# Reordering the hybrid layer's last attention units and the start of the first MLP in a two-layer diffusion backbone

## The chip, the cores and the metric

One Trainium2 chip, and of it one core. The metric is the device time of one execution in microseconds (us): a median over runs of the same program. A profile is one further execution with its own time. PE is TensorE (matmul), DVE is VectorE, ACT is ScalarE, POOL is GpSimd, SP is SyncE, whose queue issues most of the loads.

## What is computed

Two post-norm layers over 512 latent tokens and 256 context tokens, all in float32, model width 1024. Layer 0 is a hybrid mixer: one input projection, a bidirectional state-space scan (16 heads in 4 groups, chunks of 128 tokens) beside neighbourhood attention (8 heads), one output projection. Layer 1 is differential attention. Each layer then has a gated MLP with a convolution of width 3.

```python
ox, oc = hybrid_mixer(ux, uc, ...)            # layer 0: scan || attention, then w_out
hx = layer_norm(ALPHA * hx + mx[2] * ox, ln1_g, ln1_b)
fx = conv_ffn(modulate(hx, mx[3], mx[4]), w_up, conv_w, conv_b, w_down)
hx = layer_norm(ALPHA * hx + mx[5] * fx, ln2_g, ln2_b)

def conv_ffn(u, w_up, conv_w, conv_b, w_down):
    hdn = dwconv_centred(u @ w_up, conv_w, conv_b)
    val, gate = jnp.split(hdn, 2, axis=-1)
    return (jax.nn.silu(gate) * val) @ w_down
```

The shift, scale and gate vectors mx come from a vector times `ada_w` (1024 by 6144 in each layer).

## The kernel before

**Precision.** Each dense product is made of three passes in a reduced float format: a weight is loaded raw, split by `wchunk` (L152) into a high part `whi` (ACT, L172) and a low part `wlo` (raw minus high, L173, on DVE or, where `eng` is given, on POOL), and PE adds high times high, high times low and low times high. So a product over 1024 channels is 24 matmuls.

**Order.** The program is written as one stream. A planner at compile time gives each engine a fixed order: of the instructions that are ready by its own clock it takes the one written earliest, unless `tc.cur_priority` was raised around it (plus 4000 means: only when nothing else is ready; `ADA_LATER`, 100, a little later). On the chip each engine then works through its own queue in that order. Where `pe.chain` is true, each PE instruction that goes through `pe` is also tied behind the one written before it.

**Hybrid layer.** Before the loop over groups stand `dense_ssd(0)`, `dense_z(0)`, `x_rows(0)` (L878). The loop at L930 runs for g = 0 to 3; `run` (L857) alternates the generators `ssd_group(g)` (scan of group g: 12 steps, the last six one for each chunk) and `na_pair(g-1)` (six attention units of one head pair), and takes one step of a filler list in every second round: the dense work of the next group, `dense_na(g)`, `dense_z(g+1)`, for g = 3 also `early()` (transposes of finished scan rows by `prep_y`, and the first two output tiles `po`). For g = 3 the filler has priority plus 4000. `dense_z(g)` makes the gate z of group g: 6 tiles of 24 matmuls of 128x256; the last operation of each chunk in `ssd_group` (L709) multiplies by it.

An attention unit is: scores S (two heads, PE), softmax (DVE, ACT, DVE), transposes of P (PE), copies (ACT), product with V (PE). `split_qk` and `na_values` prepare Q, K and V of a pair in one buffer each.

After the loop come `rr` (the scan's RMS factor, L949 to L952), the gate rows G, and a part with an order written out by hand: the six units of pair 3 alternate with `piece()`, one step of `rest()`, which is an output tile `po` of 18 matmuls in the first ten steps. Each unit there is split in three: scores, transposes, product. Then follow the rest of the output projection and `out_att` (L996), with the layer norm.

**First MLP.** `ffn` (L1067) has 11 groups of two `up` calls each (an `up` is two weight chunks, two products for the latent and two for the context tokens, conv3 on ACT and DVE, gate, split) and `down`, which adds the product of a group to the residual Y (ev on DVE, L350, the sum on POOL, L352). Group gi = 1 also runs the affine maps of the first layer norm on the six tiles of Y (`affine`, L406, 8 POOL operations each), and `bgstep` interleaves `ada_dve` (L208): the modulation vectors of later sub-layers, accumulated on DVE (acc, L223) from 512 KB loads on the SP queue. In the kernel before, `bgstep(STEPS0)` takes five steps after each `up` of group 1 and two after later ones, `down` lags one group behind `up` until the last groups, where it lags two, and `W_POOL` puts the low parts of chunks 4 to 9 on POOL (chunk 2j+i belongs to `up(j)`).

## Time and profile before

| what | us |
|---|---|
| median of 3 runs (2025.8 to 2028.28) | 2026.2 |
| profiled execution | 2025.07 |
| its span, first to last instruction | 2023.3 |
| PE busy | 1920.8 |
| DVE busy | 1352.1 |
| ACT busy | 920.5 |
| POOL busy | 769.6 |

In the span the hybrid layer lasts to about 675, the first MLP to about 1235, the second layer's attention to about 1650, the second MLP to the end. A line of the timeline gives the start and the duration, engine, source line, operation, out<-in, shape and count; in square brackets stands the idle time of the engine before it and what ended it. S<-nKh,nQ are scores, S<-c_consts,P transposes, S<-Pt,V products with V.

### The profile page before, as it was taken

What the parts mean: (1) busy time and instruction counts of PE and PEld (TensorE: products, weight loads), DVE (VectorE), ACT (ScalarE), POOL (GpSimd) and SP (SyncE); (2) the same over time, 40 slices, a digit from 0 to 9 for tenths busy, and PEclk for the clock granted to TensorE, in tenths of its full rate; (3) what the DMA queues carried; (4) which work ended last, traced back from release to release, by engine and by line L of the source; (5) the groups of instructions that cost most, each with busy time, mean ns of one, the idle gap of its engine ahead of it and who ended that gap; (6) DMA issues with size and microseconds to landing.
All of it is one profiled execution on the core that took longest, in us unless ns stands there. A gap on an engine that the chain in (4) does not pass through costs nothing.

```text
span 2023.3 us, 31146 instructions
## 1 busy us (share of the span) xinstructions
PE 1920.8 (95%) x11928; PEld 1645.3 (81%) x11928; DVE 1352.1 (67%) x2172; ACT 920.5 (45%) x1799; POOL 769.6 (38%) x658
## 2 busy tenths in 40 slices
PE   7998999998699889999999999899999899999997
PEld 5887889887477788878888888899998788888886
DVE  3757565765556887887676667566665876655566
ACT  3545466585442732323222234656665644333332
POOL 2135224336315675444444408431115264222133
PEclk9999999999699989999999999999999999999999
DMA  9335342233422243433343342222122223323321
GB/s 314 113 114 170 110 129 76 96 117 117 155 68 88 87 135 100 130 116 115 105 144 106 104 135 86 92 73 85 55 66 68 89 64 126 104 84 104 103 96 62
DMA packets 109445, 217.59 MB, mean 108 GB/s; under 512 B 27112, under 2 KB 45904, under 8 KB 109296
## 3 DMA queue, kind: packets, MB, share of 16 engines
q1 hardware_dynamic: 95168, 187.87, 28.9%
q0 software_dynamic: 6016, 20.03, 2.8%
q10 hardware_dynamic: 8112, 7.71, 1.3%
q8 instruction: 94, 1.54, 0.3%
q14 instruction: 55, 0.45, 0.1%
HBM read 202.81 MB, written 8.55 MB: 104 GB/s over the span
## 4 chain that ended last, share of the span: by engine, by line
PE 72%; DVE 12%; DMA 4%; POOL 4%; ACT 4%; issue 3%; ACTq 0%; SPq 0%; DVEq 0%; POOLq 0%
PE fpx L328 20%; PE pdn L1122 11%; PE px L328 7%; PE fpc L328 5%; PE S L108 3%; PE po L108 3%; PE pc L328 3%; PE pz L344 3%; DVE acc L223 2%; PE pv L344 2%; DMA araw<-in_ada_w 2%; POOL y L409 2%; PE dSp L1329 2%; PE po L1005 2%; PE pk L328 2%
## 5 line engine op out<-in xcount | busy, mean ns | idle before, releaser
L172 ACT ACTIVATE whi<-raw 128x1024 fp32r<-128x1024 f32 (+1 forms) x203 | 213.4, 1056 | 443.5 <-PE fpc L328 167.2
L173 DVE TENSOR_TENSOR wlo<-raw,whi 128x1024 fp32r<-128x1024 f32 (+1 forms) x190 | 251.8, 1330 | 157.4 <-ACT whi L172 144.6
L352 POOL TENSOR_TENSOR y<-y,ev 128x512 f32<-128x512 f32 x144 | 212.5, 1495 | 185.1 <-DVE ev L350 175.2
L1122 PE MATMUL pdn<-whi,fact 128*128 128x512 f32 x880 | 273.1, 392 | 2.1 <-DVE ev L350 1.8
L328 PE MATMUL fpx<-ux,whi 128*128 128x512 f32 (+1 forms) x832 | 232.3, 363 | 8.2 <-DVE cv L1081 7.6
L328 PE MATMUL fpx<-u,whi 128*128 128x512 f32 (+1 forms) x832 | 226.5, 358 | 2.4 <-DVE cv L1081 1.5
L1122 PEld LDWEIGHTS pdn<-whi,fact 128*128 128x128 f32 x880 | 162.4, 188 | 37.2 <-DVE ev L350 2.9
L328 PEld LDWEIGHTS fpx<-ux,whi 128*128 128x128 f32 x832 | 150.3, 194 | 31.1 <-ACT whi L172 8.0
L1122 PE MATMUL pdn<-wlo,fact 128*128 128x512 f32 x440 | 170.8, 390 | 0.7 <-DVE wlo L173 0.7
L328 PEld LDWEIGHTS fpx<-u,whi 128*128 128x128 f32 x832 | 149.2, 191 | 25.1 <-ACT cv L1077 1.6
L328 PE MATMUL fpx<-ux,wlo 128*128 128x512 f32 (+1 forms) x416 | 151.1, 364 | 8.5 <-POOL wlo L173 6.6
L223 DVE SCALAR_TENSOR_TENSOR acc<-araw,condp,acc 128x512 f32<-128x512 f32 x140 | 137.4, 1002 | 24.4 <-DMA araw<-in_ada_w 24.0
L1106 POOL TENSOR_TENSOR fact<-cv,fact 128x768 fp32r<-128x768 f32 (+1 forms) x44 | 70.6, 1605 | 217.5 <-ACT fact L1105 217.5
L328 PE MATMUL fpx<-u,wlo 128*128 128x512 f32 (+1 forms) x416 | 148.8, 358 | 1.1 <-DVE wlo L173 1.1
L328 PE MATMUL px<-ux,whi 128*128 128x512 f32 x448 | 148.5, 405 | 0.0
L171 POOL TENSOR_TENSOR raw<-raw,G 128x1024 f32<-128x1024 f32 x30 | 74.4, 2482 | 193.0 <-DMA raw<-in_w_down 113.0
L1081 DVE SCALAR_TENSOR_TENSOR cv<-fpx,fcw,cv 128x511 f32<-128x511 f32 x176 | 130.3, 744 | 20.8 <-ACT cv L1077 19.6
L328 PE MATMUL fpc<-uc,whi 128*128 128x256 f32 x704 | 130.2, 283 | 0.0
L328 PEld LDWEIGHTS fpc<-uc,whi 128*128 128x128 f32 x704 | 112.6, 191 | 4.2 <-issue 0.6
L409 POOL TENSOR_TENSOR y<-y,gb 128x256 f32<-128x256 f32 x112 | 98.9, 918 | 35.2 <-PE lntp L388 28.7
L1077 ACT ACTIVATE cv<-fpx,fcw 128x512 f32<-128x512 f32 x88 | 67.8, 771 | 80.7 <-PE fpx L328 76.5
L350 DVE SCALAR_TENSOR_TENSOR ev<-pdn,G 128x512 f32<-128x512 f32 x120 | 81.3, 683 | 32.0 <-POOL y L352 18.9
(335 smaller groups left out, 4628.0 us busy)
## 6 DMA issues: line engine op xcount, KB each, us to landing
araw<-in_ada_w SPq DMA_DIRECT2D x96, 512.0 KB
raw<-in_w_up SPq DMA_DIRECT2D x88, 512.0 KB
raw<-in_w_down SPq DMA_DIRECT2D x44, 512.0 KB
E<-scr POOLq DMA_DIRECT2D x24, 512.0 KB, 5.4
raw<-in_w_dqk SPq DMA_DIRECT2D x16, 512.0 KB
raw<-in_w_qkv SPq DMA_DIRECT2D x12, 512.0 KB
raw<-in_w_out SPq DMA_DIRECT2D x12, 512.0 KB
raw<-in_w_bc SPq DMA_DIRECT2D x8, 512.0 KB
```

The lines of the kernel that those rows point to most:

```text
L108: i = f(*a, **k)
L171: nc.gpsimd.tensor_tensor(raw, raw, gate, op=OP.mult)
L172: nc.scalar.activation(hi[:, :n], raw[:, :n], AF.Copy)
L173: i = (eng or nc.vector).tensor_tensor(lo[:, :n], raw[:, :n], hi[:, :n].bitcast(F32), op=OP.subtract)
L223: nc.vector.scalar_tensor_tensor(acc[:, s], raw[:, i], cs, acc[:, s], op0=OP.mult, op1=OP.add)
L328: nc.tensor.matmul(ps, w[wi][:, kc], rhs(kc, ui), start=(i == 0), stop=(i == n - 1))
L344: nc.tensor.matmul(ps, u_dst(u, kc, ui, tt), w(kc, wi), start=(i == 0), stop=(i == n - 1))
L350: nc.vector.scalar_tensor_tensor(t, ps, r, Gh, op0=OP.mult, op1=OP.mult)
L352: eng.tensor_tensor(yh, yh, t, op=OP.add)
L409: i = nc.gpsimd.tensor_tensor(y[:, c:c + 256], y[:, c:c + 256], t[:, c:c + 256], op=op)
L1081: nc.vector.scalar_tensor_tensor(dst[:, lo:hi_], src[:, lo + d:hi_ + d], f[:, tap:tap + 1], dst[:, lo:hi_], op0=OP.mult, op1=OP.add)
L1122: nc.tensor.matmul(ps, acts[2 * gs[0] + kt][:, ui, 128 * tt:128 * tt + 128], ws[kt][wi][:, 0, o:o + 512], start=(m == 0), stop=(m == 3 * n ...
```

## The change

`dense_z(g)` moves from the end of the filler of group g-1 to the head of the filler of group g (for group 0 from the part ahead of the loop). `rr` is computed inside the last chunk step of group 3. In group 3 `na_pair` makes only units 0 to 2 of pair 2; units 3 to 5 go, split in three, to the head of the order written by hand, and `QK3` and `V3` of pair 3 are made after them. Two output tiles stand between the three units, two more before and after the scores of pair 3's first unit. In the first MLP `down` lags two groups throughout, the affine maps are written three after each `up` of group 1, `bgstep` takes three steps after each `up` of groups 1 to 3, G is made in group 2, and the chunks whose low part POOL makes are 8 to 11 in place of 4 to 9.

```diff
--- before.py
+++ after.py
@@ -44,11 +44,9 @@
 
 E_AHEAD = (0, 1, 1, 2)
 
-STEPS0 = 5
-
 ADA_LATER = 100
 
-W_POOL = ((4, 5, 6, 7, 8, 9), (4, 6, 8))
+W_POOL = ((8, 9, 10, 11), (4, 6, 8))
 D_POOL = (0, 1)
 DO_POOL = (0, 1)
 OB_POOL = (2, 4)
@@ -147,7 +145,6 @@
     W = (wf, "w")
     wring = [W]
     wcount = [0]
-    pool_wlo = [None]
 
     def wchunk(src, shape, gate=None, eng=None, rows=None, rp=None):
         n = int(np.prod(shape))
@@ -170,9 +167,7 @@
         if gate is not None:
             nc.gpsimd.tensor_tensor(raw, raw, gate, op=OP.mult)
         nc.scalar.activation(hi[:, :n], raw[:, :n], AF.Copy)
-        i = (eng or nc.vector).tensor_tensor(lo[:, :n], raw[:, :n], hi[:, :n].bitcast(F32), op=OP.subtract)
-        if eng is not None:
-            pool_wlo[0] = i
+        (eng or nc.vector).tensor_tensor(lo[:, :n], raw[:, :n], hi[:, :n].bitcast(F32), op=OP.subtract)
         return [t[:, :n].rearrange("p (a b) -> p a b", a=shape[0]) for t in (hi, lo)]
 
     def wrows(src, n, shape, eng=None):
@@ -709,6 +704,11 @@
             nc.vector.tensor_tensor(yf, yf, zs.pop((g, c)), op=OP.mult)
             nc.gpsimd.dma_start(scrY[c, :, 256 * g:256 * g + 256], yf)
             nc.scalar.activation(t1[:, 0].rearrange("p h q -> p (h q)"), yf, AF.Square, accum_out=ssq[:, c, g:g + 1])
+            if g == 3 and c == 3:
+                ssr = sp.tile([128, 6], F32, name="ssr")
+                nc.vector.tensor_reduce(ssr, ssq, axis=AX, op=OP.add)
+                nc.vector.tensor_scalar(ssr, ssr, 1.0 / D, RMS_EPS, op0=OP.mult, op1=OP.add)
+                nc.vector.tensor_scalar(rr, rsqrt_(ssr, sp), 1.0 / ALPHA, None, op0=OP.mult)
             yield
 
 
@@ -816,6 +816,8 @@
                 pe.matmul(av[hp], V[0:m, c, hp], Ss[e][1][0:m, i], start=(i == 0), stop=(i == len(chunks) - 1))
         out(av)
 
+    held = {}
+
     def na_values(v):
         V = np_.tile([128, 7, 128], F32, name="V")
         for grp in ((1, 2, 3, 5), (6, 0, 4)):
@@ -844,11 +846,12 @@
             return na_unit(*QK, V, 128 * k, k0, chunks + (5, 6), bt, lambda av: na_out(p, 128 * k, av), pool, tp_, nb, split)
         return na_unit(*QK, V, 128 * k, None, (5, 6), None, lambda av: na_out(p, 128 * k, av), pool, tp_, nb, split)
 
-    def na_pair(p, q, k, v, pools, nb=2):
+    def na_pair(p, q, k, v, pools, nb=2, n=6):
         QK = split_qk(q, k)
         V = na_values(v)
+        held[p] = QK, V
         yield
-        for u_ in range(6):
+        for u_ in range(n):
             bt = na_bias(p, u_, np_, nb) if u_ < 4 else None
             for _ in na_one(p, u_, QK, V, bt, pools[u_ % 4 % len(pools)], np_, nb):
                 pass
@@ -875,7 +878,7 @@
     PNA = (pna, "na")
     dense, densen, rows, zs = {}, {}, {}, {}
     bg[:] = [(0, w, h) for w in (2, 4, 3) for h in range(2)]
-    for _ in chain(dense_ssd(0), dense_z(0), x_rows(0)):
+    for _ in chain(dense_ssd(0), x_rows(0)):
         pass
     acts, atts, Yt, pend = {}, {}, {}, []
 
@@ -932,13 +935,11 @@
             pmm.seq = MM
         gens = [ssd_group(g, *rows[g])]
         if g > 0:
-            gens.append(na_pair(g - 1, *densen[g - 1], [(nring, None) if g == 3 else PNA]))
-        fl = []
+            gens.append(na_pair(g - 1, *densen[g - 1], [(nring, None) if g == 3 else PNA], n=3 if g == 3 else 6))
+        fl = [dense_z(g)]
         if g < 3:
             fl += [dense_ssd(g + 1), x_rows(g + 1)]
         fl.append(dense_na(g))
-        if g < 3:
-            fl.append(dense_z(g + 1))
         if g == 3:
             fl.append(early())
         run(gens, chain(*fl), 4000 if g == 3 else 0)
@@ -946,10 +947,6 @@
     pmm.seq = MM + [(pm3, "mm")]
     while bg:
         fill()
-    ssr = sp.tile([128, 6], F32, name="ssr")
-    nc.vector.tensor_reduce(ssr, ssq, axis=AX, op=OP.add)
-    nc.vector.tensor_scalar(ssr, ssr, 1.0 / D, RMS_EPS, op0=OP.mult, op1=OP.add)
-    nc.vector.tensor_scalar(rr, rsqrt_(ssr, sp), 1.0 / ALPHA, None, op0=OP.mult)
     s1.close()
     s4 = ExitStack()
     op4 = s4.enter_context(tc.tile_pool(name="op4", bufs=1))
@@ -1026,22 +1023,33 @@
         next(rs_, None)
         tc.cur_priority = pr
 
+    two = (PNA, (pss, "ax"))
+    bt2 = na_bias(2, 3, np_, 2)
+    late = [lambda k=k: na_one(2, k, *held[2], bt2 if k == 3 else None, two[k % 2], np_, 2, True) for k in (3, 4, 5)]
     bts = [na_bias(3, b, np2, 4) for b in range(2)]
-    QK3 = split_qk(*N[:2])
-    V3 = na_values(N[2])
     for tt in range(6):
         load_res(tt)
     evac_y()
     pe.chain = True
     prev = None
-    for k in range(6):
+    for n_, make in enumerate(late + list(range(6))):
+        if n_ == 3:
+            next(prev)
+            piece()
+            next(prev, None)
+            prev = None
+            QK3 = split_qk(*N[:2])
+            V3 = na_values(N[2])
+            piece()
+        k = n_ - 3
         if 0 < k < 3:
             bts.append(na_bias(3, k + 1, np2, 4))
-        un = na_one(3, k, QK3, V3, bts[k] if k < 4 else None, (PNA, (pss, "ax"))[k % 2], np2, 4, True)
+        un = make() if n_ < 3 else na_one(3, k, QK3, V3, bts[k] if k < 4 else None, two[k % 2], np2, 4, True)
         next(un)
         if prev is not None:
             next(prev)
-        piece()
+        if n_:
+            piece()
         if prev is not None:
             next(prev, None)
         prev = un
@@ -1174,20 +1182,18 @@
         if not pieces:
             G = [gate_rows(l, 1, 0, fL, "G0")]
             wring[:] = [W, W, W, W, (arp, "ar")]
+        lag = 2 if with_ctx else 1
         for gi in range(1, NG):
             for i in range(2):
                 up(2 * gi + i, 2 if gi < 2 else 1)
-                if gi == 1 and i == 0 and with_ctx:
-                    for tt in range(3):
-                        affine(Y[tt], gb, pool_wlo[0] if tt == 0 else None)
-                bgstep(STEPS0 if gi == 1 else 2)
-            if gi == 1 and pieces:
+                if gi == 1 and with_ctx:
+                    for tt in range(3 * i, 3 * i + 3):
+                        affine(Y[tt], gb)
+                bgstep(3 if gi <= 3 else 2)
+            if gi == 2 and pieces:
                 G = [gate_rows(l, 1, s, fL, f"G{s}", scaled=False) for s in range(2)]
-            if gi < NG - 2:
-                if gi == 1 and with_ctx:
-                    for tt in range(3, 6):
-                        affine(Y[tt], gb)
-                down([gi - 1])
+            if lag <= gi < NG - 3 + lag:
+                down([gi - lag])
                 bgstep(1)
         down([NG - 3])
         wring[:] = [W]
```

## Rows read from the trace of the kernel before

**Rows 1.** The page: busy time of each engine, and the clock in 40 slices.

```profile
PE 1920.8 (95%) x11928; PEld 1645.3 (81%) x11928; DVE 1352.1 (67%) x2172; ACT 920.5 (45%) x1799; POOL 769.6 (38%) x658
PEclk9999999999699989999999999999999999999999
```

**Rows 2.** Windows: length, busy us (and count) of engines, PE clock, DMA share, GB/s.

```profile
336.00:442.00 106.00, 104.31 (x698) 90.99 (x697) 72.96 (x165) 69.89 (x161) 39.55 (x52) 1.00 0.31 98
...
442.00:485.00 43.00, 42.98 (x270) 36.88 (x269) 21.45 (x41) 27.64 (x68) 17.69 (x21) 1.00 0.27 89
485.00:531.00 46.00, 36.55 (x177) 27.84 (x175) 28.56 (x66) 25.19 (x72) 28.38 (x37) 0.78 0.55 186
531.79:560.05 28.26, 14.81 (x66) 8.67 (x67) 16.57 (x29) 14.47 (x42) 7.46 (x4) 0.57 0.31 100
560.05:607.20 47.15, 47.06 (x274) 35.88 (x272) 26.51 (x62) 18.98 (x54) 9.47 (x8) 0.97 0.21 66
...
675.24:768.89 93.65, 78.12 (x624) 76.37 (x624) 73.52 (x90) 40.41 (x75) 67.88 (x58) 0.91 0.37 118
```

**Rows 3.** Windows of the same columns, cut where the granted clock is half.

```profile
535.74:563.04 27.30, 16.02 (x61) 9.92 (x60) 18.56 (x34) 13.12 (x37) 7.46 (x4) 0.50 0.29 96
...
702.99:713.23 10.24, 6.13 (x28) 6.13 (x29) 7.72 (x9) 0.00 (x0) 10.24 (x11) 0.50 0.45 154
```

**Rows 4.** Waits of PE from 685 to 860: us in total, times, longest.

```profile
PE fpx L328 <- DVE cv L1081: 7.6, 2, 7.1
PE fpx L328 <- POOL wlo L173: 6.6, 1, 6.6
```

**Rows 5.** Timeline of PE: two steps of dense_z(3), and the start of scan group 3.

```profile
430.28 0.40 PE L344 MATMUL pz<-whi,ux 128*128 128x256 f32 x2
...
430.64 0.40 PE L344 MATMUL pz<-whi,ux 128*128 128x256 f32 x2
...
442.09 0.81 PE L629 MATMUL btp<-c_consts,xc 128*128 128x128 f32 x6
```

**Rows 6.** Timeline of all engines: end of group 3, units 3 to 5 of pair 2.

```profile
524.07 0.42 DVE L709 TENSOR_TENSOR xD<-xD,zs 128x256 f32<-128x256 f32 x1
...
526.65 0.39 PE L108 MATMUL S<-nKh,nQ 128*128 128x512 f32 x1
...
531.79 0.63 PE L108 MATMUL S<-c_consts,P 128*128 128x128 f32 x4 [0.70 <-DVE rr L952]
531.86 0.80 SPq L289 DMA_DIRECT2D G<-in_ada_br  x2
...
543.55 0.56 PE L108 MATMUL S<-nKh,nQ 128*128 128x256 f32 x1
...
553.91 1.08 PE L108 MATMUL S<-c_consts,P 128*128 128x128 f32 x4 [9.29 <-DVE P L802]
```

**Rows 7.** Timeline of PE: scores of two units of pair 3 that follow each other.

```profile
580.40 0.73 PE L108 MATMUL S<-nKh,nQ 128*128 128x512 f32 x2
...
587.67 0.86 PE L108 MATMUL S<-nKh,nQ 128*128 128x256 f32 x2
```

**Rows 8.** Groups of instructions from 679 to 745: busy us, mean ns, idle before.

```profile
L409 POOL TENSOR_TENSOR y<-y,gb 128x256 f32<-128x256 f32 x48 | 44.2, 955 | 4.6 <-ACT ux L401 4.6
...
L223 DVE SCALAR_TENSOR_TENSOR acc<-araw,condp,acc 128x512 f32<-128x512 f32 x22 | 29.2, 1367 | 6.6 <-DMA araw<-in_ada_w 6.6
...
L173 POOL TENSOR_TENSOR wlo<-raw,whi 128x1024 fp32r<-128x1024 f32 x5 | 13.6, 2728 | 3.1 <-ACT whi L172 3.1
...
L1081 DVE SCALAR_TENSOR_TENSOR cv<-fpx,fcw,cv 128x511 f32<-128x511 f32 x10 | 7.2, 739 | 0.6 <-ACT cv L1077 0.5
```

**Rows 9.** Lines L223 and L173 over the span: min/median/max ns.

```profile
L223 DVE SCALAR_TENSOR_TENSOR acc<-araw,condp,acc x140: 734/748/2893, 700.2 to 1218.6; 128x512 f32<-128x512 f32 x140
...
L173 DVE TENSOR_TENSOR wlo<-raw,whi x190: 426/1224/3079, 16.6 to 1992.6; 128x1024 fp32r<-128x1024 f32 x189, 128x256 fp32r<-128x256 f32 x1
```

**Rows 10.** Timeline of DVE from 698 to 746: the accumulation that waits longest.

```profile
733.26 3.94 DVE L223 SCALAR_TENSOR_TENSOR acc<-araw,condp,acc 128x512 f32<-128x512 f32 x2 [4.10 <-DMA araw<-in_ada_w]
```

## The prediction

> **What bounds the kernel.** I read the page first: PE is busy 95% of the span, so the kernel is as long as PE's work plus the places where PE idles or runs at the lower of its two clocks; the row of clock slices shows where those are, since only few slices fall below full [rows 1]. Then the windows by stage [rows 2]: from 336 to 442 PE is busy 104.31 of 106 us at full clock, so there a microsecond of PE work removed is a microsecond gained. From 442 to 485 it is full (42.98 of 43). Then come two holes in the hybrid layer, 485 to 531 (36.55 busy at clock 0.78) and 531.79 to 560.05 (14.81 busy at 0.57), and one in the first MLP, 675.24 to 768.89 (78.12 busy at 0.91). Busy time times clock is what PE would need at full clock: 28.5 of 46, 8.4 of 28.3 and 71 of 93.7 us. The room is 17.5, 19.8 and 22.5 us. Those are the three places that the change touches, and their sum, about 60 us, is all it can gain. In cold stretches the clock is half, 1.2 instead of 2.4 GHz, each time after PE had idled or had only transposes and small products [rows 3].
>
> Who ends the waits differs. In the MLP it is a low part on POOL (6.6 us, once) and the convolution on DVE (7.6 us in two) [rows 4]. In 531.79 to 560.05 it is softmax, unit after unit, with no dense work between them [rows 6].
>
> **dense_z one group later.** A z group is 6 tiles of 24 matmuls, and three matmuls of it take 0.36 us [rows 5], so 144 x 0.12 = 17.3 us. Each group's z only changes places with the next one's, all in stretches that PE fills, except the last: z of group 3 leaves the full stretch before the start of group 3 (442.09 [rows 5]) and goes into group 3's own filler. So group 3 starts 17.3 us earlier, and the 17.3 us come back inside it, partly. The scan's own steps there are a chain over DVE, ACT and POOL, from 442.09 to the last gate at 524.07 [rows 5, 6], 82 us; the filler ranks 4000 below it. Given back could be nothing, if the 17.5 us of room after 485 takes it all, or 17.3, if everything behind it (dense_na(3), the transposes of prep_y, the first po) just slides. z must be ready before the first chunk's gate, so what slides into the room is the later filler, and prep_y needs PSUM slots that dense_na holds. The first 43 us of the group are already full [rows 2], which speaks for the slide; the 46 after it are not, which speaks against. I stand between the two rows: half comes back. **Gain 8.7, ends 0 and 17.3.** The weight loads and splits of z move with it and are the same work; cover for them on ACT and DVE in 442 to 485 is 15 and 21 us of idle time [rows 2].
>
> **rr earlier.** Now the loads of G go out 7.8 us after the last gate (531.86 against 524.07 [rows 6]). Two short tiles of statistics move ahead; the first evacuations of po come a few us earlier. I cost and gain nothing: with three PSUM slots for po the first tile between the units doesn't need it, and if it did, it would be late by less than those 7.8.
>
> **Units 3 to 5 of pair 2 in the hand-written order.** These units, V of pair 3 and the first scores are what fills 531.79 to 560.05. At full clock they are 8.4 us of PE work; the rest is wait. With a po tile between transposes and product the same units run as pair 3's do now: 7.27 us from scores to scores (580.40 to 587.67 [rows 7]), PE full from 560.05 to 607.20 [rows 2]. Split Q, K and V of pair 3 are then made under po tiles as well. No po work is added, it only moves up from the dense tail. What stays: the first unit has only the second's scores between its scores and its transposes; now that is 5.1 us (526.65 to 531.79 [rows 6]). **Gain 19.8 - 5.1 = 14.7, ends 19.8 and below zero** (a rival below prices that). The new waits stand in PE's queue: a po tile now sits ahead of each product with V and needs its transposed rows from prep_y; everything tied behind it would wait, the scores of the next unit first.
>
> **First MLP.** In group 1 POOL runs 48 affine operations at 0.955 us, 44 us, and among them low parts at 2.73 us [rows 8]; PE stood 6.6 us for one of them, and after it worked 6.13 us at half clock, 3.1 us lost [rows 3, 4]. With the low parts of chunks 4 to 7 on DVE this wait has no place: 9.7 us. The affine maps still take their 44 us, but down(0) comes one group, two up calls, later, so they stay hidden; the cover is two ups of dense work, 35 us. The other wait, 7.06 us for a convolution, came from DVE: an accumulation waited 4.10 us for its load and two then took 3.94 [rows 10], ahead of the convolution in the queue. Three steps instead of five after an up ask for 3 loads of 512 KB instead of 5 in that time, which helps; but DVE gets four low parts at 1.22 us in the median [rows 9], more while POOL is busy, so some 5 to 6 us, and the steps that left group 1 come in groups 2 and 3 (4 accumulations each), where evacuations now share DVE. So I take the first wait and not the second. **Gain 9.7, ends 22.5 and -6** (four low parts in front of convolutions, nothing gained). The last groups are untouched: there down lagged two already. The two low parts of up(5) that go to POOL take 2 x 2.7 us of an engine that has finished its affine maps by then; nothing.
>
> Accumulations take 734 ns at least, 748 in the median, and 1367 in the mean while POOL runs its maps [rows 8, 9]. The Trainium skill (SBUF — State Buffer, "SBUF: two separate sides") says why: VectorE with two SBUF inputs and GpSimd share a port pair that one instruction holds to its end while the other blocks. The rows agree. By that rule the added low parts are dearer on DVE than their median and hold up the maps in turn, which is the second rival below; on the other side each holds the pair for 1.22 and not 2.4 us.
>
> **Sum.** 8.7 + 14.7 + 9.7 = 33.1 us. The profiled execution took 2025.07, so 1992.0; the median of the runs is 1.1 higher: **1993 us**.
>
> **The rivals.**
> 1. *Group 3 just slides, and the units gain half.* The z work comes back whole (0), and the units win 7.4 (half of 14.7) because prep_y is late and po tiles wait for it. For it: the full 442 to 485. Against it: 17.5 us of room right behind. 2026.2 - 7.4 - 9.7 = **2009**.
> 2. *DVE bounds the MLP's start.* DVE is busy 73.5 of 93.65 us there [rows 2], and accumulations at 1.37 us make a step 5.5 us: six steps are 33 us, the eight convolution operations of an up at most 8 x 0.74 = 6 [rows 8], so with two ups and the four low parts DVE has 33 + 12 + 6 = 51 us against 35 of PE (an up is 48 matmuls of 512 columns and 48 of 256, 17.3 us at the 0.12 us for 256 columns [rows 5]). What hides that is that accumulations may be put off. If they are not, the MLP pays the 6 us instead of winning 9.7: 2026.2 - 23.4 + 6 = **2009**.
> 3. *The planner undoes it.* It places what is ready by its own clock; units and z may land where they were, and the low parts trade one engine's queue for another's: **2026**.
> 4. *Slower: the tied order makes PE wait at every unit.* Unit 5 took 10.36 us from scores to transposes (543.55 to 553.91 [rows 6]), as DVE did splits and gate rows in between. If all nine units go at that pace, they take 9 x 10.36 = 93 us; before it was 28.3 + 6 x 7.27 = 72. That is +21; with z sliding whole and the MLP's 9.7 it is **2038**. It decides once a unit takes longer from scores to transposes than the 7.27 us of a round; for pair 3 now it doesn't, as PE is full there [rows 2].
>
> **How the numbers follow.** Forecast 59% (1974 to 2010, with its ends), the first rival 15%, the second 13%, the third 5%, the fourth 8%. The range 1974 to 2016 takes in nine tenths of the forecast (at its low end the three rooms are filled to about nine tenths) and the first two rivals with 7 us above them, 0.53 + 0.28 = 0.81; it leaves out the third and the fourth. A measurement can tell 0.2% from no change, some 4 us. Faster by more: 0.59 + 0.15 + 0.13 = 0.87; within: 0.05; slower: 0.08.
>
> **What would show it.** The first transposes of group 3 (btp) should start at about 425 and the last gate at 508 to 516; if it is nearer 524, z came back whole. In the hand-written part no gap of PE above 3 us after the first unit, and clock 1.00 from there on; out_att should begin about 23 us earlier than now. In the MLP no PE wait for a POOL low part before up(4), and the first down product after up(5). Wrong it is if PE waits in the chain for transposed rows, if convolutions on DVE are what ends PE's waits in groups 1 to 3, or if a hole opens somewhere that is full now.

## The result, and the profile after

The changed kernel takes 2044.7 us in the median of 4 runs (2039.68 to 2047.41), the kernel before 2027.24 in its 4 (2025.8 to 2028.81): a ratio of 1.0081, 95% interval 1.006 to 1.0103. The forecast was 1993; the time moved the other way and lies outside the range. The profiled execution of after took 2047.32, its span is 2045.5.

Where the span went, cut at the same work in both kernels. The marks are starts of PE instructions read from the timelines: first transposes (btp) of scan group 3, the last gate on DVE, first product of out_att, first up product (fpx) of the first MLP, first product of the next sub-layer (dSp).

| us from the span's start | before | after | z alone | units alone | z(3) and units | z and units |
|---|---|---|---|---|---|---|
| btp of group 3 | 442.1 | 413.8 | 414.5 | 441.3 | 419.8 | 413.1 |
| last gate | 524.1 | 530.1 | 526.7 | 521.7 | 523.5 | 529.7 |
| out_att | 637.6 | 645.1 | 650.0 | 629.9 | 629.9 | 643.0 |
| first fpx | 675.2 | 684.1 | 687.7 | 668.9 | 668.8 | 681.9 |
| first dSp | 1330.1 | 1350.3 | 1346.0 | 1323.4 | 1328.2 | 1338.0 |
| end of the span | 2023.3 | 2045.5 | 2039.8 | 2016.8 | 2021.4 | 2031.0 |

Of the 22.2 us, 8.8 are lost before the first MLP, 11.4 in it (666.2 instead of 654.8 us), 2.0 behind it. The page's busy line and clock slices, of after (before: [rows 1]):

```profile
PE 1930.5 (94%) x11928; PEld 1648.5 (81%) x11928; DVE 1372.4 (67%) x2177; ACT 918.1 (45%) x1796; POOL 773.1 (38%) x656
PEclk9997999999899989999999999999999999999999
```

PE does the same 11928 matmuls and is busy 10 us longer. Slice 4 (153 to 205 us), full before, stands at 7, and slice 11 (511 to 563), at 6 before, at 8. So one cold stretch was eased and another opened 350 us ahead of it. Windows of after, columns as in [rows 2]; the first is scan group 0, then group 3 up to its gate, gate to out_att, and the MLP's first 200 us in four pieces:

```profile
97.40:175.40 78.00, 64.72 (x356) 54.16 (x355) 52.42 (x117) 39.44 (x94) 41.37 (x58) 0.80 0.36 120
...
413.80:530.10 116.30, 113.58 (x737) 97.05 (x737) 75.97 (x151) 71.59 (x178) 40.55 (x48) 0.97 0.25 81
530.10:645.10 115.00, 101.91 (x540) 77.47 (x537) 68.27 (x129) 49.95 (x131) 47.00 (x41) 0.94 0.42 139
684.10:744.10 60.00, 50.26 (x390) 49.00 (x391) 53.33 (x72) 30.01 (x60) 49.89 (x49) 0.91 0.42 130
744.10:784.10 40.00, 38.64 (x292) 35.77 (x295) 33.84 (x42) 12.34 (x17) 14.35 (x6) 1.00 0.46 141
784.10:824.10 40.00, 33.44 (x213) 28.09 (x206) 34.45 (x45) 10.55 (x15) 13.93 (x7) 1.00 0.40 120
824.10:884.10 60.00, 54.29 (x287) 44.37 (x286) 49.81 (x69) 15.58 (x20) 23.18 (x15) 0.97 0.42 123
```

The same stretches of before (group 0; group 3 up to its gate; gate to out_att):

```profile
97.40:175.40 78.00, 73.08 (x521) 62.39 (x520) 45.47 (x83) 39.15 (x75) 34.80 (x46) 0.99 0.42 135
...
442.10:524.10 82.00, 72.53 (x415) 59.61 (x414) 47.51 (x99) 50.09 (x133) 45.39 (x56) 0.88 0.38 128
...
524.10:637.60 113.50, 99.15 (x500) 73.65 (x500) 64.81 (x126) 45.62 (x121) 38.01 (x31) 0.88 0.31 104
```

Busy times mean clock is, roughly, PE's work at full clock; the rest of a window is lost. **Group 0:** 78 us held 72.3 us of work before and hold 51.8 now; 20.5 us are lost that were not (19.6 if the windows are cut where the granted clock steps). **Group 3:** lost were 18.2 of 82.0 us, now 6.1 of 116.3. The room that the prediction saw was there and is filled, for 12.1 us; it was paid for in group 0. **Gate to out_att:** 113.5 us became 115.0. Here the mean clock misleads, since PE idled most while the clock was low. Before, 16.02 of PE's 99.15 busy us lie in the stretch at 1.2 GHz from 535.74 to 563.04 [rows 3], so it did 91.1 us of work and lost 22.4. In after, 11.0 of 101.91 busy us are at 1.2 GHz, nearly all in the two windows below, so it did 96.4 and lost 18.6. So 3.8 us less are lost there, and 5.3 us more work lies behind the gate.

```profile
547.47:554.29 6.82, 4.69 (x15) 3.44 (x13) 2.63 (x5) 3.53 (x9) 3.72 (x4) 0.50 0.42 122
...
585.01:591.84 6.83, 5.98 (x18) 4.85 (x18) 3.42 (x8) 2.55 (x7) 0.42 (x1) 0.50 0.19 62
```

Waits of PE in group 0 of after, and where its z work is (tile pz: count, min/median/max ns, first and last start):

```profile
PE gp L682 <- DVE t L692: 6.2, 1, 6.2
PE adaps L188 <- DMA araw<-in_ada_w: 3.4, 2, 3.1
PE op L690 <- DVE xD L702: 2.5, 2, 2.0
```

```profile
L339 PE MATMUL pz<-whi,ux x64: 278/283/387, 68.0 to 95.4; 128*128 128x256 f32 x64
...
L339 PE MATMUL pz<-whi,ux x64: 276/283/470, 204.0 to 225.5; 128*128 128x256 f32 x64
```

z(0) runs at 68.0, ahead of group 0, where it ran before (68.7); z(1), at 181.3 to 209.7 before, runs at 204.0 to 239.0. So z(0) did not move at all, and z(1) went back by 23 us. The kernel before has no z work at all in the 78 us: what is missing there now is other dense work, the products of `dense_ssd(1)` and `dense_na(0)` (109 px matmuls of 512 columns instead of 149, 72 pc of 256 instead of 144). The scan ran ahead of it: group 1's first transposes came at 167.7 instead of 197.5, and PE waits for the scan's own steps on DVE.

In the first MLP, waits of PE over its whole length in after (us in total, times, longest):

```profile
PE fpc L323 <- DVE cv L1089: 9.0, 4, 3.3
PE pdn L1130 <- DVE ev L345: 7.8, 8, 2.2
PE fpx L323 <- DVE cv L1089: 5.0, 4, 3.5
PE lntp L383 <- ACT y L377: 5.0, 2, 3.9
```

Before, the two of [rows 4] led, and evacuations took 1.8 us. The wait for POOL's low part (6.6) is gone. In its place stand 6.4 us more for convolutions (14.0 and 7.6), 6.0 more for evacuations, and a LayerNorm wait of 5.0 at the end (0.9 before). What DVE did ahead of one of these waits, and PE's row (timelines of after, start, length, in brackets the idle time before):

```profile
795.20 0.98 DVE L1089 SCALAR_TENSOR_TENSOR cv<-fpc,fcw,cv 128x255 f32<-128x255 f32 x2
798.70 0.88 DVE L216 TENSOR_SCALAR acc<-araw,condp 128x512 f32<-128x512 f32 x2 [2.52 <-DMA araw<-in_ada_w]
799.50 1.41 DVE L218 SCALAR_TENSOR_TENSOR acc<-araw,condp,acc 128x512 f32<-128x512 f32 x2
802.44 3.07 DVE L218 SCALAR_TENSOR_TENSOR acc<-araw,condp,acc 128x512 f32<-128x512 f32 x3 [1.53 <-DMA araw<-in_ada_w]
805.44 0.74 DVE L1089 SCALAR_TENSOR_TENSOR cv<-fpx,fcw,cv 128x511 f32<-128x511 f32 x1
806.10 1.40 DVE L218 SCALAR_TENSOR_TENSOR acc<-araw,condp,acc 128x512 f32<-128x512 f32 x2
807.42 0.74 DVE L1089 SCALAR_TENSOR_TENSOR cv<-fpx,fcw,cv 128x511 f32<-128x511 f32 x1
...
808.31 0.48 PE L323 MATMUL fpc<-uc,whi 128*128 128x256 f32 x2 [3.15 <-DVE cv L1089]
```

From 796.18 to 805.44 DVE has only accumulations: 5.4 us of work and 4.05 us in which the one at the head of its queue waits for its load. The convolutions stand behind, and PE waits 3.15 us for the second. Of accumulations (L216 and L218) DVE does 96 in the first 200 us after the first fpx, against 80 before; two runs below show that this number alone doesn't decide.

### The profile page after: what moved, and what is told of

It is laid out like the page before. It is cut to its first block, busy times and chain, and to the rows that moved or that the text cites. A ratio compares the mean times of both kernels' runs of the same rounds, so it can differ in the third digit from the quotient of the medians.

```text
span 2045.5 us, 31144 instructions
## 1 busy us (share of the span) xinstructions
PE 1930.5 (94%) x11928; PEld 1648.5 (81%) x11928; DVE 1372.4 (67%) x2177; ACT 918.1 (45%) x1796; POOL 773.1 (38%) x656
## 4 chain that ended last, share of the span: by engine, by line
PE 65%; DVE 16%; DMA 6%; issue 5%; POOL 4%; ACT 4%; SPq 0%; ACTq 0%; DVEq 0%; POOLq 0%
PE fpx L323 19%; PE pdn L1130 11%; PE px L323 6%; PE fpc L323 4%; PE pc L323 3%; DVE acc L218 3%; PE po L106 3%; DMA araw<-in_ada_w 3%; PE pz L339 2%; PE S L106 2%; PE pv L339 2%; PE dSp L1335 2%; PE po L1002 2%; PE pk L323 2%; DVE wlo L170 2%
## 5 line engine op out<-in xcount | busy, mean ns | idle before, releaser
L170 DVE TENSOR_TENSOR wlo<-raw,whi 128x1024 fp32r<-128x1024 f32 (+1 forms) x192 | 256.6, 1342 | 200.1 <-ACT whi L169 187.6
L323 PE MATMUL px<-ux,whi 128*128 128x512 f32 x448 | 153.0, 417 | 1.2 <-ACT E L676 0.8
L218 DVE SCALAR_TENSOR_TENSOR acc<-araw,condp,acc 128x512 f32<-128x512 f32 x140 | 128.8, 943 | 23.9 <-DMA araw<-in_ada_w 23.4
L1089 DVE SCALAR_TENSOR_TENSOR cv<-fpx,fcw,cv 128x511 f32<-128x511 f32 x176 | 130.3, 745 | 21.5 <-ACT cv L1085 20.2
L404 POOL TENSOR_TENSOR y<-y,gb 128x256 f32<-128x256 f32 x112 | 103.4, 959 | 35.4 <-PE lntp L383 30.6
L323 PEld LDWEIGHTS px<-ux,whi 128*128 128x128 f32 x448 | 85.7, 197 | 20.5 <-ACT E L676 1.5
```

The costliest lines, as they stand in the source:

```text
L170: (eng or nc.vector).tensor_tensor(lo[:, :n], raw[:, :n], hi[:, :n].bitcast(F32), op=OP.subtract)
L218: nc.vector.scalar_tensor_tensor(acc[:, s], raw[:, i], cs, acc[:, s], op0=OP.mult, op1=OP.add)
L323: nc.tensor.matmul(ps, w[wi][:, kc], rhs(kc, ui), start=(i == 0), stop=(i == n - 1))
L404: i = nc.gpsimd.tensor_tensor(y[:, c:c + 256], y[:, c:c + 256], t[:, c:c + 256], op=op)
L1089: nc.vector.scalar_tensor_tensor(dst[:, lo:hi_], src[:, lo + d:hi_ + d], f[:, tap:tap + 1], dst[:, lo:hi_], op0=OP.mult, op1=OP.add)
```

## The experiments

Each run is compared with runs of the kernel before on the same chip; us are (ratio - 1) x 2028. Single executions of one kernel on one chip scatter by some 5 us to either side (the widest set, 35 of the kernel before, goes from 2019.75 to 2037.86), so a profile tells where time lies and the ratio how much. By the intervals, a difference between two rows of the table is uncertain by some 4 us. "Parts" are the three of the change: **z** (dense_z in its own group), **units** (pair 2's last units in hand order, with the early rr), **MLP** (lag, low parts, affine maps, steps).

| run | ratio, 95% interval | us |
|---|---|---|
| z | 1.0058 [1.0045, 1.0071] | +11.8 |
| units | 0.9951 [0.9933, 0.9969] | -9.9 |
| MLP | 0.9980 [0.9969, 0.9992] | -4.1 |
| z(3) alone, with units | 0.9978 [0.9967, 0.9990] | -4.5 |
| units and MLP | 0.9978 [0.9960, 0.9996] | -4.5 |
| z and MLP | 1.0073 [1.0058, 1.0087] | +14.8 |
| z and units | 1.0053 [1.0034, 1.0072] | +10.7 |
| all (the changed kernel) | 1.0081 [1.0060, 1.0103] | +16.4 |
| all, steps as before | 1.0043 [1.0027, 1.0059] | +8.7 |
| all, steps as before, lag 1 | 1.0041 [1.0026, 1.0056] | +8.3 |
| units and lag | 0.9986 [0.9974, 0.9998] | -2.8 |
| units and low parts | 0.9947 [0.9931, 0.9963] | -10.7 |
| units, low parts, affine maps, lag 1 | 0.9953 [0.9936, 0.9969] | -9.5 |
| the same, lag 2 | 0.9955 [0.9941, 0.9968] | -9.1 |
| all, half the modulation products | 0.9976 [0.9960, 0.9992] | -4.9 |
| before, half the modulation products | 0.9975 [0.9956, 0.9994] | -5.1 |

**The z move alone.**

```diff
-    for _ in chain(dense_ssd(0), dense_z(0), x_rows(0)):
+    for _ in chain(dense_ssd(0), x_rows(0)):
-        fl = []
+        fl = [dense_z(g)]
-        if g < 3:
-            fl.append(dense_z(g + 1))
```

> The kernel before with the gate work dense_z one group later, and nothing else of the change. Theory A (group 0 starves): z of group 0 stays where it was, since it is the only work that is ready there, and group 0's filler loses 17.3 us of PE work; in the changed kernel the stretch 97.4 to 175.4 did 64.72 x 0.80 = 52 us of full-clock PE work against 73.08 x 0.99 = 72 before, a loss of 20.6, and the two groups after it lose some 4 more; the late z gives back up to 17.5 in group 3. So slower than before by 8 to 14 us, about 2037, with PE idle and at half clock between 125 and 175. Theory B (the prediction's): faster by 8.7 (0 to 17.3), about 2018, and no idle stretch ahead of group 1.

Measured +11.8 us, theory A's size, with marks as in the changed kernel up to group 3 (the table of marks). The loss is the z move's own; no other part is needed for it.

**Only z of group 3 moved, with the units.** z(0) to z(2) stay one group ahead.

```diff
+        fl = [dense_z(3)] if g == 3 else []
-        if g < 3:
+        if g < 2:
             fl.append(dense_z(g + 1))
```

> The kernel before with the units in the hand-written order, the early rr, and of the gate work only that of group 3 moved into group 3's filler: groups 0 to 2 keep theirs. Theory A (what the z move loses is lost in group 0): nothing starves, and the move gives what was forecast, 8.7 on top of the units' 10 to 18: 2000 to 2009. Rival (group 3 just slides): the same time as the units alone, within 3 us.

Windows of this run: group 0, then group 3 up to its gate.

```profile
97.40:175.40 78.00, 73.06 (x512) 62.21 (x512) 44.62 (x83) 39.11 (x78) 34.17 (x44) 0.98 0.43 141
...
419.80:523.50 103.70, 92.19 (x561) 76.83 (x559) 62.24 (x136) 63.49 (x165) 49.83 (x62) 0.88 0.30 95
```

Where its z(3) lies (tile pz):

```profile
L344 PE MATMUL pz<-whi,ux x64: 278/283/366, 418.1 to 440.4; 128*128 128x256 f32 x64
```

With the z of groups 0 to 2 as before PE is full in group 0 (71.6 of 78), so the starvation comes from what the move does to the fillers of these groups. Whether the missing z(1) does it, or the three steps of a z(0) that is done already at the head of group 0's filler, behind which the next group's dense work is written three steps later, no run tells apart. Group 3 begins 21.5 us earlier than with the units alone, but only with its six transposes: z(3) runs from 418.1 to 441.8, where it ran before (419.4 to 442.0), and the gate comes 1.8 us later. Of 103.7 us, 22.6 are lost, more than before. So the plan left z(3) where it was, as it left z(0), and this run never put it into the room. out_att starts at 629.9 as in the units' run: the gain ahead of the MLP is zero, the rival's case. The rest of the difference to the units (+5.4) lies in the MLP (659.4 us from fpx to dSp instead of 654.6), whose code is the same.

**The units and the early rr alone.**

```diff
-    QK3 = split_qk(*N[:2])
-    V3 = na_values(N[2])
+    two = (PNA, (pss, "ax"))
+    bt2 = na_bias(2, 3, np_, 2)
+    late = [lambda k=k: na_one(2, k, *held[2], bt2 if k == 3 else None, two[k % 2], np_, 2, True) for k in (3, 4, 5)]
...
-    for k in range(6):
+    for n_, make in enumerate(late + list(range(6))):
```

> The kernel before with units 3 to 5 of pair 2 in the hand-written order and the early rr, and nothing else. Theory A (the units are a gain that another part hides): faster by 10 to 18 us, about 2013, as the stretch from the first of these units to the end of the output projection becomes dense; the prediction had 14.7. Theory B (the tied order stalls): PE waits at po tiles for transposed rows or at transposes for softmax, 10 us and more in sum, and the time is 2027 or above.

Waits of PE from the last gate to out_att in this run, and the largest of before in its stretch:

```profile
PE po L108 <- DVE ev L350: 5.6, 4, 3.0
PE S L108 <- DVE P L807: 2.5, 2, 2.3
PE S L108 <- issue: 2.3, 1, 2.3
```

```profile
PE S L108 <- DVE P L802: 10.8, 2, 9.3
```

The softmax waits fell from 10.8 to 2.5 us, and two thirds of that came back as waits of po tiles for DVE's evacuations (5.6). The granted clock was 1.2 GHz for 13.7 us (from 539.07 and from 569.79), against 27.3 before. Cut where the clock steps, 17.3 us are lost from gate to out_att instead of 22.4. out_att starts 7.7 us earlier, 2.4 of them won ahead of the gate. It is the part that pays, at the low end of theory A.

**z and units together, and a second profile of it.** The two diffs above.

> The kernel before with the z groups moved, the units in hand order and the early rr; the first MLP as before. Theory A (the units keep their gain behind the moved z; what is lost lies in the MLP): 0.58% - 0.49% of 2028, so 2029 to 2031, out_att's first product 4 to 5 us later than the 637.6 of before. Theory B (with the z groups slid whole into the last group there is less to gain): 2034 to 2038, out_att at 645 to 648 as in the changed kernel, and the MLP's stretch at 655 to 658 us.

> The run with z and units again, for a second profile: the first profiled execution (2032.8) was the shortest of six with a median of 2038.4. Theory A (the units' gain before out_att is lost in most executions): about 2038, out_att at 647 to 650 instead of 643.0. Theory B (it is the MLP or a later stretch that varies): out_att at 642 to 645 and the MLP's stretch at 660 or more instead of 656.1.

+10.7 in the runs, where the parts add to +1.9. The profiles don't show it: first fpx came at 681.9 and 683.1 (z alone: 687.7), the span ended at 2031.0 and 2037.5 (2039.8). Of the second profile's 6.5 us over the first, 1.2 lie before fpx, 3.4 in the MLP (659.5 and 656.1) and 1.9 after it. So in the profiles the units still win 5.8 and 4.6 us ahead of the MLP, and what takes them back isn't seen in one place. The profiled executions are also far from typical: 2041.58 is the longest of six of z alone, 2032.76 the shortest of six here. The first run's total is theory B's, its out_att (643.0) nearer to theory A's; the second run fits neither of its theories. This stays open.

**The MLP part alone.**

```diff
-W_POOL = ((4, 5, 6, 7, 8, 9), (4, 6, 8))
+W_POOL = ((8, 9, 10, 11), (4, 6, 8))
...
+        lag = 2 if with_ctx else 1
-                bgstep(STEPS0 if gi == 1 else 2)
+                bgstep(3 if gi <= 3 else 2)
...
-                down([gi - 1])
+            if lag <= gi < NG - 3 + lag:
+                down([gi - lag])
```

> The kernel before with the first MLP's part of the change alone: lag of two, affine maps and steps spread, low parts of chunks 4 to 7 on DVE and of 10 and 11 on POOL. Theory A (DVE sets the pace of groups 1 to 3): in the changed kernel the stretch of these groups lost 31 us of full-clock PE work against 26 before and the tail some 3 more, so slower by 5 to 10 us, about 2034, with PE waiting for convolutions and evacuations on DVE. Theory B (the prediction's): faster by 9.7 (-6 to 22.5), about 2017, and the loss belongs to what the hybrid layer hands over.

-4.1 us: neither theory's size. In its profile the MLP's stretch took 656.1 us against 654.8 of before, so the gain isn't seen there. PE no longer waits for a low part on POOL (6.6 before); the longest waits of the stretch are now

```profile
PE pdn L1122 <- DVE ev L350: 4.7, 5, 1.4
PE fpx L328 <- DVE cv L1081: 4.4, 3, 2.4
PE adaps L229 <- POOL y L409: 3.2, 1, 3.2
PE lntp L388 <- ACT y L382: 3.0, 1, 3.0
```

**Units and MLP; z and MLP.** Two diffs each, of those above.

> The kernel before with the units in hand order, the early rr and the whole first-MLP part; the z groups stay where they were. Theory A (the parts add): the units alone gave -9.9 and the MLP alone -4.2 on 2027.4, so 2013 (2009 to 2017), with the time from the first up product to the first product of the next sub-layer at 655 to 657 us as in the MLP run. Theory B (the MLP's planned order breaks when the units stand in front of it, as in the changed kernel, where that stretch took 666 us): 2023 to 2032. Since z is all that is left out, A would put the whole interaction (+20 us) on z together with the MLP.

> The kernel before with the z groups moved and the whole first-MLP part, the units as before. Theory A (the parts add): +11.7 - 4.2 on 2028, so 2035 (2032 to 2038). Theory B (the MLP's planned order comes out worse behind a z-moved front as in the changed kernel, where the stretch from the first up product to the next sub-layer took 666 us): 2040 to 2050, with that stretch over 660 us.

Both times are theory B's. The MLP part, -4.1 by itself, costs +5.4 behind the units, +3.0 behind z, and +5.7 behind both (16.4 - 10.7). The stretch from fpx to dSp took 656.1, 658.1, 665.3 and 666.2 us. The same source gives four plans: of the 672 DVE instructions of this stretch in the changed kernel, 549 at most can be found in the same order in the MLP run (compared by operation, tiles and shape). Behind z, DVE does 80 accumulations in the first 200 us, as many as before, and the stretch takes 665.3 us all the same, so their number alone doesn't make it long.

**The steps undone in the changed kernel.**

```diff
-                bgstep(3 if gi <= 3 else 2)
+                bgstep(5 if gi == 1 else 2)
```

> The changed kernel with the modulation steps of the loop over groups as before: 5 steps after each up of group 1 and 2 after the others, instead of 3 up to group 3 and 2 after. Theory A (the accumulations that the changed kernel places earlier fill VectorE and make TensorE wait between 60 and 200 us after the first up product): 96 accumulations in the first 200 us fall to some 80 to 90 and the time falls by 4 to 12 us, to 2033 to 2041. Theory B (the planner places the accumulations by due times, and the calls only set their program order): within 2 us of 2044.7.

The window that answers 784.10:824.10 of after, and its accumulations in the first 200 us (84 of L218 and 12 of L216 in after):

```profile
786.50:826.50 40.00, 39.40 (x230) 33.41 (x229) 25.65 (x37) 12.48 (x17) 11.42 (x6) 1.00 0.39 119
```

```profile
L218 DVE SCALAR_TENSOR_TENSOR acc<-araw,condp,acc 128x512 f32<-128x512 f32 x79 | 73.4, 970 | 10.4 <-DMA araw<-in_ada_w 10.4
...
L216 DVE TENSOR_SCALAR acc<-araw,condp 128x512 f32<-128x512 f32 x12 | 11.1, 958 | 0.0
```

-7.7 us against the changed kernel. PE is full where it lost 6.6 us, with DVE busy 25.7 instead of 34.5 of 40 us; over the 200 us there are 91 accumulations instead of 96. The time is theory A's, the number is not quite; the run with the units, the MLP part and these steps has 91 as well, and its stretch takes 654.4 us. Without the spread steps the MLP part is -2.0 behind z and units.

**Half of the modulation products.** One line, in the changed kernel and in the kernel before:

```diff
-                    else:
+                    elif (l, w) == (0, 5) or i == 0:
```

> The changed kernel with half of the modulation products of the later sub-layers left out (of each pair of channel blocks that VectorE accumulates only the first; the pieces of the first MLP's gate stay whole), so its output isn't the reference's: this prices the accumulations. Theory A (they set the pace of the MLP in the changed kernel): 12 to 25 us faster than the changed kernel, and more than the same omission gives in the kernel before. Theory B (the loss of the MLP lies at its start and end, with DMA or GpSimd): under 6 us faster, as much as in the kernel before.

> The kernel before with the same half of the modulation products left out. Theory A: the accumulations lie beside TensorE's work but for a few waits at the start of the MLP: 2 to 8 us faster than before, well below what the omission gives in the changed kernel. Theory B: the same gain in both kernels.

-21.3 us in the changed kernel (from +16.4 to -4.9), -5.1 before; both land on the same time. The MLP's stretch falls from 666.2 to 647.4 and from 654.8 to 649.4. PE's waits from 782 to 885 in the first, which are 12.3 us in after from 784 to 885, are one:

```profile
PE fpx L323 <- DVE cv L1089: 1.3, 1, 1.3
```

Both are theory A's. So half of the accumulations cost the path 5 us in the kernel before, and 21 as the changed kernel orders them; without that half the MLP's loss of 11.4 us is gone (647.4 against 649.4). The omission gives the planner another order as well, so this is the price of the accumulations together with the order that they bring.

**The changed kernel's profile again.**

> The changed kernel again, for a second profile: the first profiled execution (2047.3) was one of two long ones beside 2039.7 and 2042.1. Theory A (its MLP's waits at convolutions behind accumulations belong to the planned order): the stretch from the first up product to the next sub-layer again at 664 to 668 us. Theory B (they come from transfers that arrived late in that one execution): 657 to 662 us with a total of 2040 to 2042.

The stretch took 668.5 us (666.2 in the first profile; theory A, and 0.5 above its range), with the same waits at the same places; PE's from 684 to 885 begin

```profile
PE fpc L323 <- DVE cv L1089: 7.1, 3, 3.2
PE fpx L323 <- DVE cv L1089: 5.4, 4, 3.5
```

So the loss belongs to the order and not to one execution's transfers.

**Lag or low parts, with the units.** Low parts: the W_POOL line above alone. Lag:

```diff
-                down([gi - 1])
+            if lag <= gi < NG - 3 + lag:
+                down([gi - lag])
```

> The kernel before with the units in hand order, the early rr, and of the first MLP's changes the lag of two groups alone (low parts, the behind-argument and steps as before). Theory A (the lag takes the wait of the first down product off TensorE and is what gained in the MLP run): 3 to 8 us under the units alone, 2010 to 2015, with 15 to 20 us of later down products packed in 1270 to 1290. Theory B (the lag only moves TensorE's wait to the end, where the evacuations of the down products then stand closer together): within 3 us of the units alone (2017.5).

> The kernel before with the units in hand order, the early rr, and of the first MLP's changes the list of the chunks whose low parts GpSimd takes alone ((8, 9, 10, 11) instead of (4 to 9)). Theory A (two low parts net on VectorE more, about 1.2 us each, in a stretch that it fills to nine tenths, and four of them early): 0 to +6 us against the units alone, 2017 to 2024. Theory B (TensorE's wait for GpSimd's low parts, 6.6 us in [rows 4], goes): -3 to -7, 2010 to 2015.

The lag alone takes back 7.1 of the units' 9.9 us, against both theories. Its waits of PE in the MLP:

```profile
PE fpx L328 <- DVE cv L1096: 12.4, 3, 8.2
PE pdn L1137 <- DVE ev L350: 6.1, 6, 1.7
PE lntp L388 <- ACT y L382: 4.1, 2, 3.4
PE fpx L328 <- POOL wlo L173: 2.8, 1, 2.8
```

The list of low parts moves the time by -0.8 us, inside both intervals and between the theories, though no PE wait for a POOL low part is left in the MLP. In its profile, the shortest of six executions, the MLP's stretch took 649.6 us instead of 654.6, so a gain of a few us isn't ruled out. (With this list the first affine map is also no longer tied behind a low part on POOL.) With the units alone that wait had already shrunk from 6.6 to 2.8 us and the convolutions' had grown from 7.6 to 9.9.

**Steps as before, lag two and lag one.** With the spread steps a lag of one can't be had: the gate's rows aren't ready for the first down product. So the steps are as before in all of these, with the units (first two) and in the changed kernel (third; its lag of two is the run with the steps undone).

```diff
-        lag = 2 if with_ctx else 1
+        lag = 1
...
-            if gi == 2 and pieces:
+            if gi == 1 and pieces:
```

> The kernel before with the units in hand order, the early rr, and the first-MLP part but for the modulation steps, which stay 5 after each up of group 1 and 2 after the others. Theory A (the spread steps place accumulations ahead of convolutions on VectorE; undoing that gave -6.5 in the changed kernel): 6 us under the run with units and whole MLP part (2024.5), so 2018 (2014 to 2021), no better than the units alone (2017.5). Theory B (what the units and the MLP part cost each other lies in the lag or in the low parts on VectorE): 2022 to 2027.

> The kernel before with the units in hand order, the early rr, the new list of low parts and the affine maps spread over the ups of group 1, with a lag of one and the steps as before. Beside the run with a lag of two (ratio 0.9955) it tells the price of the lag in front of a z that stays. Theory A (the lag costs): 0.991 to 0.994. Theory B (it costs nothing): 0.994 to 0.997.

> The changed kernel with its down projection lagging one group and with the modulation steps as before (with a lag of one the gate's rows need them): of the MLP's changes the low parts' list and the affine maps remain. Beside the run with the steps undone alone (2038.2) it tells the price of the lag behind a moved z. Theory A (the lag costs, as the +7 to +10 of units and lag alone): 2028 to 2033. Theory B (the lag costs nothing once the affine maps and low parts are moved too): 2036 to 2040.

Lag two against lag one: -9.1 and -9.5 with the units, +8.7 and +8.3 behind z and units; theory A for the first run, B for the other two. Where the affine maps and the low parts are moved too, the lag does nothing that the runs can tell, though in both pairs of profiles the MLP's stretch is longer with lag two (654.4 and 650.6, 656.5 and 651.5).

## Why the prediction was wrong

**dense_z.** The step that failed is "Each group's z only changes places with the next one's, all in stretches that PE fills, except the last". z(0) had nothing to change places with. It was ready before group 0, so the plan left it there, and group 0's filler was one z shorter with nothing in return: PE lost 20.5 us there that it had not lost. The ends "0 and 17.3" left a loss out because the argument looked only at the group that z leaves last. What it said of group 3 held in part: the room of 17.5 us is filled, by 12.1, when group 3 is given 46 us more work at full clock (110.2 instead of 63.8). z(3) alone did not go there: with the other z as before the plan kept it at 418.1 to 441.8, ahead of the scan's steps, so its worth inside group 3 stays unmeasured. Term: a gain of 8.7 forecast, a loss of 11.8 measured.

**rr.** Forecast at nothing; it was not run by itself, and is in the units' number.

**Units.** The mechanism was right: the waits for softmax went from 10.8 to 2.5 us. The size was off: 14.7 forecast, 9.9 measured. The 5.1 us kept back for the first unit were too little, since a wait for evacuations of po (5.6 us) took part of the place, and the clock, forecast at 1.00 behind the first unit, fell twice. In the changed kernel a third kind of wait appears, the one that the first rival named: 3.3 and 2.1 us for transposed rows on ACT and 1.2 for their load.

```profile
PE ytp L106 <- ACT yr L898: 3.3, 1, 3.3
PE po L106 <- DVE ev L345: 2.5, 3, 1.3
PE S L106 <- issue: 2.3, 1, 2.3
PE po L106 <- ACT yr L898: 2.1, 1, 2.1
PE ytp L106 <- DMA yr<-scrY: 1.2, 1, 1.2
```

**First MLP.** "I take the first wait and not the second", 9.7 us, failed as a step. With the MLP part alone the wait for POOL's low part went, as forecast, but waits for evacuations (4.7 us; 1.8 before), for an affine map on POOL (3.2; none) and for a LayerNorm (3.0; 0.9) came in its place, and the gain is 4.1. The list of low parts was run only with the units, where that wait was 2.8 us: 0.8. The second rival had the right mechanism (accumulations ahead of convolutions) for the MLP behind the other two parts, with too small a price: 6 us in the prediction, 11.4 in the profile. It counted the added low parts beside them; the runs show 7.7 us for the spread steps and nothing clear of the noise for the low parts. That three steps an up instead of five would help is the part of the argument that points the wrong way behind z and units: they spread into groups 2 and 3, and DVE there has convolutions and evacuations to do. In the groups of instructions of the first 200 us the 14 low parts on DVE took 1402 ns in the mean (1340 before) and the accumulations 944 (1075); so dearer operations, as the Trainium skill's rule of the shared port pair (SBUF — State Buffer, "SBUF: two separate sides") would have them, are not what made the MLP longer.

**The sum.** The parts alone give +11.8 - 9.9 - 4.1 = -2.2 us, the whole +16.4. Of the 18.6 between, 9.8 are the MLP part, which turns from -4.1 to +5.7 behind the other two; undoing the steps takes 7.7 of them away. The other 8.8 are z and units, and open. The prediction added terms as if each stage's order were its own. The third rival (the planner undoes it) was the nearest in kind, as z(0) and the lone z(3) stayed where they were, and had no price for an order that comes out worse.

**What it had named as signs.** btp of group 3 at "about 425" came at 413.8, and the last gate, 508 to 516, at 530.1; out_att, forecast about 23 us earlier, came 7.5 later. All three signs of being wrong came: PE waits in the chain for transposed rows (above), "convolutions on DVE are what ends PE's waits in groups 1 to 3" is what the profile shows, and "a hole opens somewhere that is full now" is group 0.

**The best version.** The units with the early rr, with or without the low parts' list: 2017.5 us (0.9951) and 2018.0 (0.9947) against 2027.4 and 2028.9 of before on their chips. Nothing that was added to them gained more that the runs can tell.

## What to carry to other kernels

Before moving filler from one stage to the next, ask what the first stage gets in return: work that is ready early stays early, and the stage behind it starves. Look in the trace whether the moved work moved at all; z(0), and z(3) when it was moved alone, did not. Judge a step of background work by what stands behind it in the engine's queue, above all when it waits for a load at the head of it. Where a planner orders the code, run parts alone and together: the same source came out 10 us longer behind another prologue.

## What had not been expected of the hardware

One wait of PE in group 0 cost more than its own length. Windows of after, cut where the granted clock fell and rose:

```profile
138.00:151.52 13.52, 10.04 (x56) 8.40 (x54) 5.02 (x9) 7.26 (x21) 8.24 (x14) 1.00 0.60 175
151.52:175.41 23.89, 17.47 (x55) 14.09 (x56) 22.27 (x56) 12.00 (x33) 11.70 (x17) 0.50 0.20 65
```

The wait of 6.15 us began at 148.04; inside it, at 151.52, the granted clock went from 2.4 to 1.2 GHz, and it stayed there for 21 us after PE went on at 154.19, through 17.47 us of work. At full clock this work would have taken half, so up to 8.7 us were lost beside the 6.15, in a stretch where PE still had work for three quarters of the time. How much of the 8.7 PE would then have spent waiting for DVE instead isn't shown.
